# Hybrid encoder trunk on one core: two-half score products, recurrent scans one per attention step, post-norms with the gain first

## The chip, the cores and the metric

The kernel runs on one core of a Trainium2 chip. The core has a matrix engine (TensorE, "PE" in the profile, with its weight loads as "PEld"), three engines for elementwise work (VectorE "DVE", ScalarE "ACT", GpSimd "POOL"), a fifth engine that issues transfers (SyncE "SP"), an on-chip memory of 128 partitions (SBUF) and eight accumulation banks of 128 x 512 floats that PE writes (PSUM). The metric is the device time of one execution in microseconds. Three runs of the kernel before took 1062.80 to 1063.61 us, median 1063.17.

## The reference

An encoder of two layers, 512 tokens of 1024 channels, all in float32. Every layer does `x += post_norm(mixer(pre_norm(x)))` and then `x += post_norm(SwiGLU(pre_norm(x)))`, with RMS norms. Layer 0 mixes by differential attention beside a recurrent branch, layer 1 by a two-dimensional Fourier transform and a linear map. The parts that the change touches:

```python
def rmsnorm(x, g):
    y = x * rsqrt(mean(x * x, axis=-1) + EPS) * g

def diff_attention(q, k, v, lam, ...):       # 4 heads, two 64-wide parts each
    s = einsum('bqhmd,bkhmd->bhmqk', qi, k) * 64 ** -0.5
    p = softmax(s - slopes * dist, axis=-1)
    a = p[:, :, 0] - lam * p[:, :, 1]        # then a @ v and a norm per head

def rg_lru(x, w_a, b_a, w_i, b_i, lam, reverse):   # forward and backward, 512 channels
    r, i = sigmoid(gate products of x)
    a = exp(8 * r * log_sigmoid(lam))
    u = sqrt(1 - a * a) * (i * x)
    h = scan(h = a * h + u)                  # along the 512 positions

rec = (h_fwd + h_bwd) * gelu(yg)
out = concat([attn, rec]) @ w_out
```

## The kernel before

Every large product is made from split operands. A float32 tensor is divided into a high part with a short mantissa (a cast) and a low part (the rest, a subtraction), and a product is three matrix products: high by high, high by low and low by high (`mm3`, lines 108 to 111). `split` (lines 100 to 106) makes the two parts, by default with the cast on ACT and the subtraction on DVE. The weights come as "units" of 256 columns or rows, two halves of 512 KB each: a transfer into one of three raw buffers on SP's queue, a cast, a subtraction (`prep_half`). For units 8 to 13 the subtraction is on POOL. All large tiles, weights included, share 33 slots of 4 KB a partition.

The order in which each engine works is not the program's. A planner orders the instructions of every engine by a priority that follows the program's order, with its own estimate of when operands are ready and slots come free; `order_after` adds an edge that only fixes the order. All engines then work through their queues in order.

Layer 0 goes as follows. After the first norm come the products for the values, the recurrent branch's input with its convolution, and the gates. `lru_decay` (lines 503 to 514) and `lru_root` (518 to 521) make the scans' two inputs for 8 pairs of direction and channel block; the last multiplication of each is on POOL (line 521). `proj_qk(0)` (lines 538 to 567) makes queries and keys of heads 0 and 1, each in four halves of 12 products. A head's query product is a bank whose partitions 0 to 63 hold part 0 and partitions 64 to 127 part 1.

In the kernel before, the split of queries and keys stacks the parts. For queries and each part m, one tile holds the high part in the 64 partitions of m and the low part in the other 64 (lines 555 to 557). For keys, one tile holds the high part twice, and a third tile `klo` holds the low part (lines 561 to 565). A score block is then, for each of the two parts, one product over 128 rows (high by high plus low by high) and one over 64 rows (high by low), lines 582 and 583.

The attention runs in 16 steps, head by head, four blocks of 128 queries each (lines 712 to 722). A step does `scores`; half of a projection (`next(fill)`: queries and keys of heads 2 and 3 in steps 0 to 7, the GELU branch's input in steps 8 to 15); two scans in each of steps 0 to 3; and in `finish_step` the transposes of the mixed probabilities of two steps earlier, the product with the values for a pair of older blocks, and the norm of an older head. In `scores`, DVE scales the bank, adds the position bias and takes the row maximum in one operation (line 585), negates the maximum (587), ACT takes the exponent with the sum (588), and DVE mixes the two parts (592). The backward scan of a channel block is followed by a sum on POOL (line 530); `take_yg`, after the steps, uses that sum.

`proj_tok` makes the products whose result has tokens in the partitions (the mixers' output and the FFN's second product), block by block, with `finish` after each block. There `post_norm` (lines 256 to 267) squares both halves on ACT with a row sum, forms the root's argument on DVE and the root on POOL (`inv_rms`, `inv_sqrt`), and then does per half a product with root and gain (line 266) and the sum into x (line 267) on DVE. In the last FFN, `after1` sends both halves of a finished block to memory from SP.

Of the kernel before, what the change touches and what calls it, by code (L numbers as in the profile page):

```python
# [16 lines left out]
P = 128  # L17
D = 1024
S = 512
# [16 lines left out]
def encoder_kernel(  # L36
# [167 lines left out]
    make_identity(nc, ident)  # L204
    mhalf = const.tile([P, 4], F32, name="mhalf")
    V.memset(mhalf, -0.5)

    def inv_sqrt(m):
        r = sm("r")
        G.tensor_tensor(out=r, in0=m, in1=mhalf[:, 0:1], op=ALU.pow)  # L210
        return r

    def inv_rms(ssa, ssb, n):

        m0, m = sm("m"), sm("m")
        V.tensor_scalar(out=m0, in0=ssa, scalar1=n * EPS, scalar2=None, op0=ALU.add)
        V.tensor_scalar(out=m, in0=ssb, scalar1=m0, scalar2=1.0 / n, op0=ALU.add, op1=ALU.mult)  # L217
        return inv_sqrt(m)

    def pre_stats(t, junk):  # L220
        ss = [sm("ss"), sm("ss")]
        for h in range(2):
            A.activation(junk[h], xt[t][:, h * S:(h + 1) * S], AF.Square, accum_out=ss[h])
        return inv_rms(ss[0], ss[1], D)
# [31 lines left out]
    def post_norm(t, ps, g):  # L256
# [3 lines left out]
        for h in range(2):  # L260
            A.activation(ys[h], ps[h], AF.Square, accum_out=ss[h])  # L261
        r = inv_rms(ss[0], ss[1], D)
        for h in range(2):
            sl = slice(h * S, (h + 1) * S)
            y = ys[h]
            V.scalar_tensor_tensor(out=y, in0=ps[h], scalar=r, in1=g[:, sl], op0=ALU.mult, op1=ALU.mult)
            V.tensor_tensor(out=xt[t][:, sl], in0=xt[t][:, sl], in1=y, op=ALU.add)
# [255 lines left out]
    def lru_scan(d, c):  # L523
        a_, q, u = lru_ac.pop((d, c))
        if d == 0:
            V.tensor_tensor_scan(out=u, data0=a_, data1=u, initial=0.0, op0=ALU.mult, op1=ALU.add)
            hsum[c] = u
        else:
            V.tensor_tensor_scan(out=u[:, ::-1], data0=a_[:, ::-1], data1=u[:, ::-1], initial=0.0, op0=ALU.mult, op1=ALU.add)
# [8 lines left out]
    def proj_qk(h0):  # L538

        qh = {}  # L540
        for z in range(2):
            u = next_unit(1)
            for h in (h0, h0 + 1):
# [8 lines left out]
                a = pair("qk", F32R)  # L552
                if z == 0:

                    for m, sl in enumerate(halves):
                        A.copy(a[m][sl, :], ps[sl, :])
                        V.tensor_tensor(out=a[m][halves[1 - m], :], in0=ps[sl, :], in1=f(a[m][sl, :]), op=ALU.subtract)
                    qh[h] = a
                else:

                    lo = tile1k("klo", F32R)[:, 0:S]
                    for m, sl in enumerate(halves):
                        A.copy(a[m][sl, :], ps[sl, :])
                        A.copy(a[m][halves[1 - m], :], ps[sl, :])
# [391 lines left out]
```

## Time and profile before

| what | value |
|---|---|
| median of three runs | 1063.17 us (1062.80 to 1063.61) |
| the profiled execution's own time | 1063.37 us |
| its span, first to last instruction | 1061.6 us |
| PE busy | 1040.4 us (98%) |
| DVE busy | 487.3 us (46%) |
| ACT busy | 391.7 us (37%) |
| POOL busy | 99.4 us (9%) |
| transfers | 102.40 MB, mean 96 GB/s |

The profile shows one execution. A group of instructions is named by its source line, engine and operation, then output and inputs by the program's names; after the bar come busy time and the mean duration in ns, then idle time ahead of it and what ended that. Matrix products are pipelined: their listed durations overlap, so the distance from start to start tells what one costs. A table of stages gives, per stretch of time, each engine's busy microseconds with the number of its instructions in brackets, then the share of full TensorE clock that was granted, the busy share of the DMA engines and the transfer rate.

### The profile page before, as it was taken

Reading aid. Unit: us, or ns where it says so; the run is one execution under the profiler, and the core shown is the slowest. Engines: PE = TensorE matmul, PEld = TensorE weight load, DVE = VectorE, ACT = ScalarE, POOL = GpSimd, SP = SyncE. Lnnn points to the kernel's source line nnn. Section 1 sums busy time; section 2 is a strip of 40 time slices with the busy share of each in tenths; the row PEclk is TensorE's granted clock in tenths of the full one; section 3 lists DMA queues with packets and bytes.
Section 4 is the critical chain, followed back from the end, with each engine's and each line's share of the span. In section 5 each row is a group of like instructions: output and inputs, shape, how many; then the busy total and the mean of one; then the engine's idle time right before and its main releaser. Section 6 shows DMA issues by size and latency. Waiting matters only on the chain.

```text
span 1061.6 us, 12308 instructions
## 1 busy us (share of the span) xinstructions
PE 1040.4 (98%) x4927; PEld 862.0 (81%) x4927; DVE 487.3 (46%) x763; ACT 391.7 (37%) x645; POOL 99.4 (9%) x94
## 2 busy tenths in 40 slices
PE   8997999999999999999999999999999999999997
PEld 7885677779888888888888888898888888888885
DVE  6869987755542322223324456545322223234304
ACT  5377567743531321122223445334321123223202
POOL 1057424211000000000100110100000000000000
PEclk9998999999999999999999999999999999999999
DMA  6432212321652243222443015027243223324002
GB/s 218 125 103 91 75 48 75 117 80 41 179 177 80 80 135 103 80 80 79 152 127 119 1 60 159 1 70 221 88 126 111 80 79 105 94 80 128 11 1 79
DMA packets 72981, 102.40 MB, mean 96 GB/s; under 512 B 3878, under 2 KB 61275, under 8 KB 72924
## 3 DMA queue, kind: packets, MB, share of 16 engines
q1 hardware_dynamic: 70298, 93.49, 28.2%
q0 software_dynamic: 2624, 8.13, 2.3%
q8 instruction: 38, 0.62, 0.2%
q14 instruction: 19, 0.16, 0.0%
q10 hardware_dynamic: 2, 0.00, 0.0%
HBM read 99.51 MB, written 2.10 MB: 96 GB/s over the span
## 4 chain that ended last, share of the span: by engine, by line
PE 86%; DVE 8%; ACT 3%; issue 1%; DMA 1%; POOL 0%; SPq 0%; DVEq 0%; POOLq 0%; ACTq 0%
PE pc L109 15%; PE pc L110 15%; PE pc L111 15%; PE pj L111 10%; PE pj L110 10%; PE pj L109 10%; DVE wlo L106 2%; ACT gate L93 1%; PE psc L583 1%; DVE xc L430 1%; PE pyg L109 1%; DMA raw<-in_w_in_dram 1%; PE pT L251 1%; PE psc L582 1%; PE put L110 1%
## 5 line engine op out<-in xcount | busy, mean ns | idle before, releaser
L106 DVE TENSOR_TENSOR wlo<-raw,whi 128x1024 fp32r<-128x1024 f32 x158 | 191.8, 1238 | 269.9 <-ACT whi L103 218.3
L110 PE MATMUL pc<-hnlo,whi 128*128 128x512 f32 (+1 forms) x768 | 285.2, 372 | 0.0
L109 PE MATMUL pc<-hnhi,whi 128*128 128x512 f32 (+1 forms) x768 | 284.6, 372 | 0.5 <-ACT hnhi L103 0.5
L111 PE MATMUL pc<-hnhi,wlo 128*128 128x512 f32 (+1 forms) x768 | 285.0, 371 | 0.0
L103 ACT CAST whi<-raw 128x1024 fp32r<-128x1024 f32 x164 | 167.3, 1050 | 116.7 <-PE pj L110 31.1
L110 PEld LDWEIGHTS pc<-hnlo,whi 128*128 128x128 f32 x768 | 144.7, 188 | 25.5 <-DVE hnlo L106 0.4
L109 PEld LDWEIGHTS pc<-hnhi,whi 128*128 128x128 f32 x768 | 144.2, 188 | 25.7 <-ACT hnhi L103 1.0
L111 PEld LDWEIGHTS pc<-hnhi,wlo 128*128 128x128 f32 x768 | 144.7, 188 | 24.9
L109 PE MATMUL pj<-whi,gs 128*128 128x512 f32 x352 | 136.9, 389 | 0.0
L111 PE MATMUL pj<-whi,gs 128*128 128x512 f32 x352 | 136.9, 389 | 0.0
L110 PE MATMUL pj<-wlo,gs 128*128 128x512 f32 x352 | 136.9, 389 | 0.0
L93 ACT ACTIVATE gated<-pc 128x512 f32<-128x512 f32 x44 | 26.2, 597 | 271.6 <-PE pc L111 271.6
L753 DVE TENSOR_TENSOR gated<-gated,pc 128x512 f32<-128x512 f32 x44 | 30.2, 686 | 112.3 <-PE pc L111 112.3
L110 PEld LDWEIGHTS pj<-wlo,gs 128*128 128x128 f32 x352 | 66.1, 188 | 13.8
L109 PEld LDWEIGHTS pj<-whi,gs 128*128 128x128 f32 x352 | 66.1, 188 | 13.8
L111 PEld LDWEIGHTS pj<-whi,gs 128*128 128x128 f32 x352 | 66.1, 188 | 13.5
L210 POOL TENSOR_TENSOR r<-m,mhalf 128x1 f32<-128x1 f32 x32 | 17.4, 545 | 551.0 <-DVE m L217 544.5
L261 ACT ACTIVATE y<-pj 128x512 f32<-128x512 f32 x32 | 19.1, 596 | 82.3 <-PE pj L111 82.3
L103 ACT CAST gs<-gated 128x512 fp32r<-128x512 f32 x44 | 25.3, 619 | 52.2 <-PE pj L110 32.2
L106 DVE TENSOR_TENSOR gs<-gated,gs 128x512 fp32r<-128x512 f32 x44 | 28.4, 685 | 31.0 <-ACT gs L103 31.0
L106 POOL TENSOR_TENSOR wlo<-raw,whi 128x1024 fp32r<-128x1024 f32 x12 | 29.5, 2471 | 49.7 <-ACT whi L103 48.6
L93 ACT ACTIVATE p<-p,mx 128x512 f32<-128x512 f32 x32 | 23.1, 723 | 22.4 <-DVE mx L587 22.3
(199 smaller groups left out, 1299.3 us busy)
## 6 DMA issues: line engine op xcount, KB each, us to landing
raw<-in_w_ffn_gate_dram SPq DMA_DIRECT2D x44, 512.0 KB, 4.6
raw<-in_w_ffn_up_dram SPq DMA_DIRECT2D x44, 512.0 KB, 5.0
raw<-in_w_ffn_down_dram SPq DMA_DIRECT2D x44, 512.0 KB, 3.3
raw<-in_w_in_dram SPq DMA_DIRECT2D x20, 512.0 KB, 4.6
raw<-in_w_mix_out_dram SPq DMA_DIRECT2D x8, 512.0 KB, 3.2
raw<-in_w_fourier_out_dram SPq DMA_DIRECT2D x8, 512.0 KB, 3.7
pos<-in_dft_pos_dram POOLq DMA_DIRECT2D x8, 256.0 KB, 6.3
out_dram<-x SPq DMA_DIRECT2D x8, 256.0 KB, 2.1
```

The source lines that it names most:

```text
L93: ins = A.activation(out_, in_, func, **kw)
L103: A.copy(hi, src)
L106: lo_eng.tensor_tensor(out=lo, in0=src, in1=f(hi), op=ALU.subtract)
L109: T.matmul(ps, lhsT=l[0], rhs=r[0], start=start, stop=False)
L110: T.matmul(ps, lhsT=l[0], rhs=r[1], start=False, stop=False)
L111: T.matmul(ps, lhsT=l[1], rhs=r[0], start=False, stop=stop)
L210: G.tensor_tensor(out=r, in0=m, in1=mhalf[:, 0:1], op=ALU.pow)
L251: T.transpose(pt[:, k * P:(k + 1) * P], xh[:, k * P:(k + 1) * P], ident)
L261: A.activation(ys[h], ps[h], AF.Square, accum_out=ss[h])
L430: V.scalar_tensor_tensor(out=y[:, o], in0=ps[:, i_], scalar=cw[:, k * 4 + c:k * 4 + c + 1], in1=y[:, o], op0=ALU.mult, op1=ALU.add)
L582: T.matmul(ps, lhsT=q_[m][:, t * P:(t + 1) * P], rhs=k_[m], start=True, stop=False)
L753: V.tensor_tensor(out=gated[fc], in0=gated[fc], in1=ps, op=ALU.mult)
```

## The change

Queries and keys are split like every other operand: one cast on ACT and one subtraction on DVE over all 128 partitions, no third tile. The score block becomes six products over 64 rows. For each of the three terms, the product of part 0 (partitions 0 to 63) is followed by that of part 1 (partitions 64 to 127), and the two parts accumulate in two banks taken together. The reduction takes a negative scale and the minimum, so that the exponent can use the result without the negation.

Of the scans, one is done in each of steps 1, 2, 4, 5, 7, 8, 10 and 11, with an edge that puts it behind the last score reduction made so far on DVE.

The root's argument gets its 1/D by the scale of the square. `post_norm` multiplies by the gain first, from the bank, and then does one operation per half that multiplies by the root and adds x. The square's elementwise output goes to a fixed tile, `junk`. The second half of every output block is issued from ACT's queue.

```diff
+    RD = 1.0 / math.sqrt(D)
+    def inv_rms(ssa, ssb):
+        m0, m, r = sm("m"), sm("m"), sm("r")
+        V.tensor_scalar(out=m0, in0=ssa, scalar1=EPS, scalar2=None, op0=ALU.add)
+        V.tensor_tensor(out=m, in0=ssb, in1=m0, op=ALU.add)
         G.tensor_tensor(out=r, in0=m, in1=mhalf[:, 0:1], op=ALU.pow)
...
         for h in range(2):
-            A.activation(ys[h], ps[h], AF.Square, accum_out=ss[h])
-        r = inv_rms(ss[0], ss[1], D)
+            V.tensor_tensor(out=ys[h], in0=ps[h], in1=g[:, h * S:(h + 1) * S], op=ALU.mult)
+            A.activation(junk, ps[h], AF.Square, scale=RD, accum_out=ss[h])
+        r = inv_rms(ss[0], ss[1])
         for h in range(2):
             sl = slice(h * S, (h + 1) * S)
-            y = ys[h]
-            V.scalar_tensor_tensor(out=y, in0=ps[h], scalar=r, in1=g[:, sl], op0=ALU.mult, op1=ALU.mult)
-            V.tensor_tensor(out=xt[t][:, sl], in0=xt[t][:, sl], in1=y, op=ALU.add)
+            V.scalar_tensor_tensor(out=xt[t][:, sl], in0=ys[h], scalar=r, in1=xt[t][:, sl], op0=ALU.mult, op1=ALU.add)
...
+            sc = V.tensor_tensor_scan(out=u, data0=a_, data1=u, initial=0.0, op0=ALU.mult, op1=ALU.add)
...
+        order_after(sc, [last_score[0]])
+        if d:
             G.tensor_tensor(out=hsum[c], in0=hsum[c], in1=u, op=ALU.add)
...
                 a = pair("qk", F32R)
+                split(*a, ps)
                 if z == 0:
-                    for m, sl in enumerate(halves):
-                        A.copy(a[m][sl, :], ps[sl, :])
-                        V.tensor_tensor(out=a[m][halves[1 - m], :], in0=ps[sl, :], in1=f(a[m][sl, :]), op=ALU.subtract)
                     qh[h] = a
                 else:
-                    lo = tile1k("klo", F32R)[:, 0:S]
-                    for m, sl in enumerate(halves):
-                        A.copy(a[m][sl, :], ps[sl, :])
-                        A.copy(a[m][halves[1 - m], :], ps[sl, :])
-                        V.tensor_tensor(out=lo[sl, :], in0=ps[sl, :], in1=f(a[m][sl, :]), op=ALU.subtract)
-                    qks[h] = (qh[h], a, lo)
+                    qks[h] = (qh[h], a)
...
+        ps = [bank("psc"), bank("psc")]
+        for n, (i, j) in enumerate(((0, 0), (0, 1), (1, 0))):
+            for m, sl in enumerate(halves):
+                T.matmul(ps[m], lhsT=q_[i][sl, t * P:(t + 1) * P], rhs=k_[j][sl, :], start=n == 0, stop=n == 2)
         for m in range(2):
-            sl = halves[m]
-            ps = bank("psc")
-            T.matmul(ps, lhsT=q_[m][:, t * P:(t + 1) * P], rhs=k_[m], start=True, stop=False)
-            T.matmul(ps, lhsT=q_[m][sl, t * P:(t + 1) * P], rhs=klo[sl, :], start=False, stop=True)
-            mx = sm("mx")
-            V.tensor_tensor_reduce(out=pr[m], in0=ps, in1=bias[h][:, 384 - t * P:384 - t * P + S],
-                                   op0=ALU.add, op1=ALU.max, scale=1.0 / math.sqrt(QK), scalar=-3.0e38, accum_out=mx)
-            V.tensor_scalar(out=mx, in0=mx, scalar1=-1.0, scalar2=None, op0=ALU.mult)
-            act(pr[m], pr[m], AF.Exp, "exp", bias=mx, accum_out=s_[:, m * NT + t:m * NT + t + 1])
+            mn = sm("mn")
+            last_score[0] = V.tensor_tensor_reduce(out=pr[m], in0=ps[m], in1=bias[h][:, 384 - t * P:384 - t * P + S],
+                                   op0=ALU.add, op1=ALU.min, scale=-1.0 / math.sqrt(QK), scalar=3.0e38, accum_out=mn)
+            act(pr[m], pr[m], AF.Exp, "exp", scale=-1.0, bias=mn, accum_out=s_[:, m * NT + t:m * NT + t + 1])
...
+    scans = list(lru)
     for i in range(n):
...
-        if 2 * i < len(lru):
-            lru_scan(*lru[2 * i])
-            lru_scan(*lru[2 * i + 1])
+        if i % 3 and scans:
+            lru_scan(*scans.pop(0))
...
-        for h in range(2):
-            nc.sync.dma_start(out[t * P:(t + 1) * P, h * S:(h + 1) * S], xt[t][:, h * S:(h + 1) * S])
+        for h, q in enumerate((nc.sync, A)):
+            q.dma_start(out[t * P:(t + 1) * P, h * S:(h + 1) * S], xt[t][:, h * S:(h + 1) * S])
```

More of the change, by code (lines that the diff above doesn't have):

```diff
@@ L204, in encoder_kernel @@
     make_identity(nc, ident)
+    junk = const.tile([P, S], F32, name="junk")
     mhalf = const.tile([P, 4], F32, name="mhalf")
     V.memset(mhalf, -0.5)
-    def inv_sqrt(m):
-        r = sm("r")
+    RD = 1.0 / math.sqrt(D)
[3 more added lines that the diff above has]
+        V.tensor_tensor(out=m, in0=ssb, in1=m0, op=ALU.add)
         G.tensor_tensor(out=r, in0=m, in1=mhalf[:, 0:1], op=ALU.pow)
         return r
[L213 to L218, printed above, removed]
     def pre_stats(t, junk):
@@ L222, in pre_stats @@
         for h in range(2):
-            A.activation(junk[h], xt[t][:, h * S:(h + 1) * S], AF.Square, accum_out=ss[h])
-        return inv_rms(ss[0], ss[1], D)
+            A.activation(junk[h], xt[t][:, h * S:(h + 1) * S], AF.Square, scale=RD, accum_out=ss[h])
+        return inv_rms(ss[0], ss[1])
     hn = {}
@@ L525, in lru_scan @@
         if d == 0:
-            V.tensor_tensor_scan(out=u, data0=a_, data1=u, initial=0.0, op0=ALU.mult, op1=ALU.add)
+            sc = V.tensor_tensor_scan(out=u, data0=a_, data1=u, initial=0.0, op0=ALU.mult, op1=ALU.add)
             hsum[c] = u
         else:
-            V.tensor_tensor_scan(out=u[:, ::-1], data0=a_[:, ::-1], data1=u[:, ::-1], initial=0.0, op0=ALU.mult, op1=ALU.add)
+            sc = V.tensor_tensor_scan(out=u[:, ::-1], data0=a_[:, ::-1], data1=u[:, ::-1], initial=0.0, op0=ALU.mult, op1=ALU.add)
+        order_after(sc, [last_score[0]])
+        if d:
             G.tensor_tensor(out=hsum[c], in0=hsum[c], in1=u, op=ALU.add)
@@ L570, in encoder_kernel @@
     sums = {}
+    last_score = [None]
     def scores(h, t):
-        q_, k_, klo = qks[h]
+        q_, k_ = qks[h]
         pr = pair("p")
```

## The prediction

> **What bounds the kernel now.** I read the page's engine totals and the chain of waits first.
>
> ```profile
> PE 1040.4 (98%) x4927; PEld 862.0 (81%) x4927; DVE 487.3 (46%) x763; ACT 391.7 (37%) x645; POOL 99.4 (9%) x94
> ...
> PE 86%; DVE 8%; ACT 3%; issue 1%; DMA 1%; POOL 0%; SPq 0%; DVEq 0%; POOLq 0%; ACTq 0%
> ```
>
> The matrix engine (PE) has work in 98% of the span and carries 86% of the chain. So only two things can move the time: a stretch where PE stands still, or fewer PE microseconds where it is dense. The table of stages shows where it stands still.
>
> ```profile
> core 0: us, PE busy (x) PEld busy (x) DVE busy (x) ACT busy (x) POOL busy (x), PEclk, DMA share, GB/s
> 85.00:95.00 10.00, 10.00 (x45) 8.07 (x43) 9.88 (x14) 9.58 (x16) 8.35 (x5) 1.00 0.19 53
> 95.00:105.00 10.00, 3.50 (x9) 1.96 (x8) 9.91 (x8) 3.83 (x7) 10.00 (x5) 0.74 0.17 53
> 105.00:115.00 10.00, 10.00 (x28) 6.09 (x28) 9.94 (x13) 5.59 (x9) 5.80 (x4) 0.75 0.17 53
> 115.00:125.00 10.00, 8.52 (x34) 5.59 (x33) 9.07 (x20) 3.54 (x8) 4.70 (x4) 1.00 0.39 144
> ```
>
> Up to 95 us PE is dense. From 95 to 125 it runs 9, 28 and 34 instructions in 10 us each, against 45 before, while VectorE (DVE) is busy 9.9, 9.9 and 9.1 of 10 us; the granted clock falls to 0.74 (before 1.00). The attention's sixteen steps (a step is one head and one block of 128 queries) begin at 94.74; step 4 begins at 125.90 and the last of the 32 full score products (two a step) starts at 191.0 (first and last start in the second fence below). The same table cut there, with two later stages:
>
> ```profile
> 94.74:125.90 31.16, 22.70 (x74) 14.06 (x72) 30.07 (x40) 13.67 (x25) 20.76 (x12) 0.84 0.24 82
> 125.90:190.60 64.70, 64.70 (x312) 47.99 (x309) 49.15 (x136) 44.77 (x96) 22.00 (x10) 1.00 0.21 66
> 225.00:265.00 40.00, 39.76 (x243) 35.30 (x242) 21.81 (x44) 14.62 (x37) 4.98 (x9) 1.00 0.09 27
> 680.00:710.00 30.00, 29.76 (x208) 27.53 (x207) 14.79 (x30) 9.42 (x23) 2.75 (x5) 1.00 0.06 18
> ```
>
> So DVE bounds steps 0 to 3 (30.07 of 31.16 us); in steps 4 to 15 PE is dense and DVE at 76%. PE's longest wait between 90 and 230 us, and the start of the first step:
>
> ```profile
> PE psc L583 <- DVE klo L565: 5.8, 2, 3.2
> ```
>
> ```profile
> 94.74 0.39 PE L582 MATMUL psc<-qk,qk 128*128 128x512 f32 x1
> 98.38 0.50 PE L583 MATMUL psc<-klo,qk 64*128 64x512 f32 x1 [3.25 <-DVE klo L565]
> ...
> 125.90 0.47 PE L582 MATMUL psc<-qk,qk 128*128 128x512 f32 x1
> ```
>
> ```profile
> L582 PE MATMUL psc<-qk,qk x32: 388/494/628, 94.7 to 191.0; 128*128 128x512 f32 x32
> ```
>
> PE starts the first score product at 94.74 and gets the second at 98.38, waiting for the low part of the keys (klo) on DVE. What fills DVE there:
>
> ```profile
> L526 DVE TENSOR_TENSOR_SCAN gate<-gate 128x512 f32<-128x512 f32 x4 | 8.8, 2196 | 0.0
> ...
> L529 DVE TENSOR_TENSOR_SCAN gate<-gate 128x512 f32<-128x512 f32 x4 | 7.2, 1797 | 0.0
> ...
> L585 DVE CUSTOM_DVE_ANT_0 p<-psc,bias 128x512 f32<-128x512 f32 x6 | 4.0, 682 | 0.1
> L592 DVE SCALAR_TENSOR_TENSOR p<-p,c 128x512 f32<-128x512 f32 x2 | 3.6, 1795 | 0.0
> ...
> L565 DVE TENSOR_TENSOR klo<-pqk,qk 64x512 fp32r<-64x512 f32 x4 | 2.8, 688 | 0.1
> ...
> L587 DVE TENSOR_SCALAR mx<-mx 128x1 f32<-128x1 f32 x6 | 0.9, 144 | 0.0
> ```
>
> ```profile
> L526 DVE TENSOR_TENSOR_SCAN gate<-gate x4: 1199/2260/3062, 95.3 to 111.7; 128x512 f32<-128x512 f32 x4
> ```
>
> The eight recurrent scans (L526, L529) take 8.8 + 7.2 = 16.0 us, half of the stretch. One takes 1.2 us at best, 2.2 mostly; GpSimd (POOL) works in most of that time:
>
> ```profile
> 86.65 16.33 POOL L521 TENSOR_TENSOR gate<-gate,th 128x512 f32<-128x512 f32 x8 [8.01 <-ACT th L93]
> 102.94 3.42 POOL L530 TENSOR_TENSOR gate<-gate,gate 128x512 f32<-128x512 f32 x2
> 106.31 2.38 POOL L106 TENSOR_TENSOR wlo<-raw,whi 128x1024 fp32r<-128x1024 f32 x1
> ```
>
> And the score block of step 9, on PE:
>
> ```profile
> 154.81 0.60 PE L604 MATMUL paT<-ident,p 128*128 128x128 f32 x4
> 155.17 0.48 PE L582 MATMUL psc<-qk,qk 128*128 128x512 f32 x1
> 155.58 0.50 PE L583 MATMUL psc<-klo,qk 64*128 64x512 f32 x1
> 156.01 0.50 PE L582 MATMUL psc<-qk,qk 128*128 128x512 f32 x1
> 156.44 0.50 PE L583 MATMUL psc<-klo,qk 64*128 64x512 f32 x1
> 156.87 0.50 PE L109 MATMUL pyg<-hnhi,whi 128*128 128x512 f32 x1
> 157.21 0.39 PE L110 MATMUL pyg<-hnlo,whi 128*128 128x512 f32 x1
> 157.43 0.39 PE L111 MATMUL pyg<-hnhi,wlo 128*128 128x512 f32 x1
> ```
>
> Full products follow each other at 0.22 to 0.23 us (157.21 to 157.43). The four score products of a step alternate between 128 and 64 rows, and each start comes 0.41 to 0.43 after the one before; the product behind them is late too (0.34). From 155.17 to 157.21 are 2.04 us for five products, 1.15 at 0.23: 0.89 us goes to four changes of shape, 0.22 each, and a step's score block costs 2.04 - 0.23 = 1.81 us.
>
> **The change, part by part.** The sum is made against the profiled execution: 1063.37 us, of which 1061.6 is span and 1.77 lies around it; the median of the runs is 1063.17, 0.2 lower.
>
> *Score products.* Six products of 64 rows replace two full and two of 64 rows, in the order upper half, lower half, three times. The trace has no two 64-row products of different halves next to each other, so the block is bounded by rows. Two changes of shape remain (in and out, 0.22 each: 0.44). Low end: the halves run together and each pair costs a full product, 3 x 0.23 + 0.44 = 1.13 us, 0.68 less than now. If a pair runs together but the next load on the same half stays exposed, as the loads at 155.58 to 156.44 are, a pair costs 0.43: 3 x 0.43 + 0.11 (the rest of the way out, 0.34 - 0.23) = 1.40, 0.41 less. Nothing together, loads hidden: 6 x 0.23 + 0.44 = 1.82, the same as now. High end: nothing together and every load exposed: 6 x 0.43 + 0.11 = 2.69, 0.88 more. I take 1.27, between the first two, since both halves of the array are free for each other and write different banks.
>
> The Trainium skill, TensorE: Matmul & The Clock Gate, Part 3, says that a weight load overlaps a running product only where the row groups differ. The loads of full products above do overlap (the next product starts after 0.23), so the trace limits that rule; by it the block would be 1.40, by the rows of full products 1.13, and the sum below 1.6 us worse or better over twelve steps.
>
> *Splits of queries and keys.* Per head, DVE goes from four 64-partition operations (0.69 each, L565; a full-width one costs the same) to two, ScalarE (ACT) from six copies to two. Before 94.74 PE is dense, so that part only shortens DVE's backlog; the keys' low part is then one operation, due before PE ends the projections. The wait of 3.2 us at 98.38 and its twin (5.8 in two) lose their cause.
>
> *Scans.* Two at each of steps 0 to 3 become one at each of steps 1, 2, 4, 5, 7, 8, 10, 11, each behind that step's score reductions on DVE. Behind a scan now stand the step's exponent mix (L592) and the transposed copies, which PE wants two steps later. The backward scans' sums on POOL (102.94, two in 3.42) move with them: the low parts of the next key weights (106.31), behind them on POOL until now, come earlier; the gates that want the sums come after step 15, four steps after the last one. No DMA is issued by a moved operation. The backward gates' four tiles, of 33 that the weights share, stay until step 11 instead of 3, while the four of the keys' low parts are no longer taken: even.
>
> *Negations.* L587 (0.14 each, 32 of them) goes; ACT takes the sign into its scale. It is DVE time and a link between reduction and exponent.
>
> *Steps 0 to 3.* PE needs 4 x 1.27 + 48 projection products x 0.23 = 11.0 + two groups of transposes of 0.36 = 16.8 us. DVE keeps 30.1 - 16.0 = 14.1, gets two scans at 2.0 (POOL's multiplications run to 103) = 4.0 and one more step's reductions and mix (2 x 0.68 + 0.70, L592 undisturbed, as L266 below) = 2.1, and loses three splits of 0.69 and six negations (0.9) = 3.0: 17.2. Two engines near 17 with hand-overs between them make about 19: **12.2 us saved** of 31.2. Bounds: 14.9 (PE alone at block 1.13: 16.3) and 6 (a first turn that still waits, 25).
>
> *Steps 4 to 15.* PE falls by 12 x 0.54 = 6.5 from 64.7 to 58.2. DVE falls from 49.2 by two key splits, one query split (2.1) and 24 negations (3.5) to 43.6 and gets six scans at 1.2 to 2.2; POOL is busy a third of the time (22.0 of 64.7), so 1.55: 9.3, together 52.9. All scans lie in steps 4 to 11, where DVE has 8/12 of 43.6 + 9.3 = 38.4 against PE's 38.8. So near a tie costs something: I give back 1.5 us. **5.0 saved**; bounds 8.2 and, at block 2.69, a loss of 10.6.
>
> *Post-norms.* The order of multiplications changes, so that one DVE operation per half is left after the root in place of two. In the three inner ones PE's products cover it: PE lacks 0.24 us in each of the stages at 225 and 680 above, so nothing is gained, and if the cover went it would be a gain of 1.3 each at most. The last one is bare:
>
> ```profile
> 1051.19 0.60 ACT L261 ACTIVATE y<-pj 128x512 f32<-128x512 f32 x1 [1.97 <-PE pj L111]
> ...
> 1051.50 1.28 DVE L267 TENSOR_TENSOR x<-x,y 128x512 f32<-128x512 f32 x2
> ...
> 1053.97 0.60 ACT L261 ACTIVATE y<-pj 128x512 f32<-128x512 f32 x1 [2.09 <-PE pj L111]
> ...
> 1055.62 1.41 DVE L266 SCALAR_TENSOR_TENSOR y<-pj,r,gpost 128x512 f32<-128x512 f32 x2 [0.72 <-POOL r L210]
> 1056.95 1.28 DVE L267 TENSOR_TENSOR x<-x,y 128x512 f32<-128x512 f32 x2
> ```
>
> After the root (1055.62) four operations end at 1058.23; two, at 0.64 to 0.70 each, end at 1056.9: **1.3 us saved**. The early multiplications fit in the 2.7 us between the two squares (1051.19, 1053.97).
>
> *Output on two queues.* Half of each block now goes out from ACT's queue, whose one DMA issue in the trace took 0.50 us:
>
> ```profile
> 0.73 0.50 ACTq L130 DMA_DIRECT2D grow<-in_ln_mix_pre_dram  x1
> ```
>
> Behind that issue, which waits for DVE (1052.78 for block 2), stands ACT's square of the next block (1051.19); it may be late by a microsecond, covered by the one at 1053.97, which ends the block. The halves come 0.64 us apart, so a second queue has nothing to overlap: 0, bounds -0.6 and +0.5.
>
> Sum: 12.2 + 5.0 + 1.3 = 18.5; 1063.4 - 18.5 = **1045 us**.
>
> **Rivals.** (1) The halves do not run together, loads hidden: block 1.82. Steps 0 to 3: PE 19.0, about 20.2 with hand-overs, 11 saved; steps 4 to 15 nothing; tail 1.3: 1051. For it: no row shows concurrent products. Against it: nothing in the program ties the halves.
> (2) DVE becomes the bound through step 11, the scans at 2.2 with POOL beside them: a scan step needs 43.6/12 + 2.2 = 5.8 us against PE's 4.85, six times 0.98 = 5.9 in place of my 1.5, and about 3 more at the start, where hand-overs then follow each scan: 18.5 - 4.4 - 3 = 11.1, 1052. For it: the median scan of 2.26. Against it: POOL's busy third.
> (3) Slower: every 64-row load stays exposed, block 2.69, because the array empties at each change of half as at each change of shape now. Steps 0 to 3: 22.5 of PE and 3 of hand-overs, 5.6 saved; steps 4 to 15 lose 10.6; tail 1.3: +3.7, **1067**. The sign turns at a block of 2.46 (at x the change is 4x - 16.4 + 12x - 21.7 - 1.3). For it: all the exposed loads above. Against it: those follow a change between whole array and half.
> (4) The change doesn't reach the queue: the planner's order still puts other DVE work ahead of the first reductions, and steps 0 to 3 save 6 only: 1051.
>
> **How the numbers follow.** Forecast 0.58, (1) 0.15, (2) 0.1, (3) 0.07, (4) 0.1. The forecast's own spread is 1039 (14.9 + 8.2 + 1.3 = 24.4) to 1050; (1), (2) and (4) lie at 1051 and 1052, and (1) with the bound of 6 at the start comes to 1056. Range **1039 to 1057**. Faster by over 0.2% (2.1 us, about what a measurement tells from no change) 0.89, all but (3) less 0.04 for mixtures of it that end within 0.2%; slower 0.07.
>
> **What would show it.** In the table of stages, PE dense from 95 us on, the clock at 1.00, step 4 starting near 114 and step 15 ending near 173. In the timeline of a dense step, six score products with the pair's starts close together and a block of 1.1 to 1.4 us. No wait of PE for the keys' low part. Scans one at a time behind L585, DVE at 90% of those steps. Two DVE operations after the last root. I am wrong if the block is 1.8 or more, or if PE shows waits for DVE or for free banks in steps 1 to 11.

## The result and the profile after

The changed kernel takes 1050.84 us (median of four runs, 1050.56 to 1051.33) against 1063.39 us (1062.80 to 1064.03) beside it: a ratio of 0.9882 with a 95% interval of 0.9865 to 0.9899. The profiled execution took 1050.92 us, of which 1049.1 is span: 12.5 less than the 1061.6 of before. First the engine totals and the chain of the page after.

```profile
PE 1031.0 (98%) x4959; PEld 857.8 (82%) x4959; DVE 477.8 (46%) x723; ACT 382.1 (36%) x629; POOL 96.2 (9%) x94
...
PE 88%; DVE 6%; ACT 3%; issue 1%; DMA 1%; POOL 1%; SPq 0%; POOLq 0%; DVEq 0%; ACTq 0%
```

They hardly differ from those of before: PE has 9.4 us less work, and 88% of the chain. The table of stages, in three slices of the prediction, says where the time went.

```profile
95.00:105.00 10.00, 10.00 (x48) 6.75 (x47) 7.75 (x13) 6.92 (x12) 10.00 (x7) 1.00 0.30 87
105.00:115.00 10.00, 10.00 (x52) 7.35 (x50) 8.91 (x21) 4.40 (x13) 2.73 (x4) 1.00 0.44 163
115.00:125.00 10.00, 8.76 (x50) 6.44 (x49) 9.93 (x17) 5.01 (x11) 4.81 (x2) 1.00 0.33 100
```

From 95 to 115 PE runs 48 and 52 instructions where it ran 9 and 28, and the clock stays at 1.00. At 115 the picture turns: PE 8.76 of 10 us, DVE 9.93. The same table cut at the starts of steps 0, 4, 12 and 15, for the kernel before (steps 4, 12, 15) and after (steps 0, 4, 12, 15):

```profile
125.90:172.19 46.29, 46.29 (x223) 34.28 (x221) 36.88 (x103) 32.20 (x70) 11.49 (x5) 1.00 0.14 46
172.19:190.19 18.00, 18.00 (x91) 13.55 (x90) 12.27 (x34) 12.16 (x26) 10.51 (x5) 1.00 0.38 118
```

```profile
94.67:111.31 16.64, 16.64 (x81) 11.63 (x81) 14.03 (x26) 9.41 (x18) 12.69 (x10) 1.00 0.45 153
111.31:157.57 46.26, 42.93 (x237) 32.62 (x236) 40.39 (x83) 26.23 (x60) 14.56 (x8) 1.00 0.15 46
157.57:178.76 21.19, 18.17 (x97) 14.07 (x96) 16.03 (x32) 13.39 (x30) 11.83 (x6) 0.94 0.29 100
```

Steps 0 to 3 took 31.16 us and take 16.64: 14.5 saved. Steps 4 to 11 took 46.29 and take 46.26: nothing saved, though their products are shorter. Steps 12 to 14 took 18.00 and take 21.19: 3.2 lost, at a mean clock of 0.94. From step 15 to the end it was 1061.6 - 190.19 = 871.4 and is 1049.1 - 178.76 = 870.3: 1.1 saved. With 0.1 for the earlier first step these make the 12.5.

The score block itself came out as short as hoped. In PE's timeline of step 1:

```profile
98.60 0.39 PE L111 MATMUL pqk<-hnhi,wlo 128*128 128x512 f32 x1
98.92 0.97 PE L578 MATMUL psc<-qk,qk 64*128 64x512 f32 x6
99.81 0.50 PE L109 MATMUL pqk<-hnhi,whi 128*128 128x512 f32 x1
100.15 0.40 PE L110 MATMUL pqk<-hnlo,whi 128*128 128x512 f32 x1
```

Six products fill 0.97 us. From 98.60 to 100.15 are 1.55 us with two full products in them (L111 and L109, 0.23 each): the block costs 1.09, against 1.81 before. At 0.72 less in each of eleven steps, steps 4 to 14 would have gone from 64.29 to 56.4 us, had nothing else changed. They take 67.45. So 11 us were lost there, and PE's waits between 94 and 180 us name one place:

```profile
PE poT L110 <- DVE aT L106: 6.1, 3, 3.0
```

The waits for the keys' low part are gone. In their place PE waits three times, 3.0 us at the longest, with the product of transposed probabilities and values (`poT`) for DVE's low part of these probabilities (`aT`). The chain of waits from 111 to 178 us, by line, for before and after:

```profile
by line: PE psc L583 11.4%; PE psc L582 8.9%; PE pyg L109 8.4%; PE pyg L111 6.9%; PE pyg L110 6.8%; PE pqk L109 6.7%; PE paT L604 6.2%; PE pqk L110 5.5%; PE pqk L111 5.5%; DVE gate L529 5.1%; DVE p L592 4.3%; DVE p L585 3.9%; PE poT L109 3.
```

```profile
by line: DVE p L588 17.4%; DVE p L582 12.5%; ACT p L93 10.8%; DVE aT L106 9.4%; ACT whi L103 7.0%; DVE gate L525 6.1%; issue 4.7%; POOL r L628 4.4%; DVE c L587 3.7%; POOL wlo L106 3.6%; ACT oT L630 3.4%; DVE s L624 2.7%; DVE qk L106 2.3%; A
```

Before, PE's own products led that chain. After, it is DVE's: the mix (L588) leads with 17.4%, ahead of the score reductions (L582). What the mix does there, in the timelines of POOL, DVE and PE ahead of the two longest of the three waits:

```profile
120.01 2.42 POOL L106 TENSOR_TENSOR wlo<-raw,whi 128x1024 fp32r<-128x1024 f32 x1 [1.25 <-ACT whi L103]
...
120.18 2.79 DVE L588 SCALAR_TENSOR_TENSOR p<-p,c 128x512 f32<-128x512 f32 x1
...
126.07 1.32 POOL L532 TENSOR_TENSOR gate<-gate,gate 128x512 f32<-128x512 f32 x1 [3.65 <-DVE c L586]
...
126.27 1.67 DVE L588 SCALAR_TENSOR_TENSOR p<-p,c 128x512 f32<-128x512 f32 x1
...
128.46 0.68 DVE L106 TENSOR_TENSOR aT<-paT,aT 128x512 fp32r<-128x512 f32 x1
...
129.19 0.39 PE L110 MATMUL poT<-aT,v 128*128 128x256 f32 x1 [2.02 <-DVE aT L106]
...
167.34 7.06 POOL L106 TENSOR_TENSOR wlo<-raw,whi 128x1024 fp32r<-128x1024 f32 x3 [2.19 <-ACT whi L103]
...
172.15 2.81 DVE L588 SCALAR_TENSOR_TENSOR p<-p,c 128x512 f32<-128x512 f32 x1
...
174.88 0.68 DVE L106 TENSOR_TENSOR aT<-paT,aT 128x512 fp32r<-128x512 f32 x1
...
175.61 0.39 PE L110 MATMUL poT<-aT,v 128*128 128x256 f32 x1 [3.02 <-DVE aT L106]
```

A mix takes 0.75 us alone. Here two take 2.79 and 2.81, and end at 122.97 and 174.96: 0.54 and 0.56 us after POOL's subtraction of weights has ended (122.43 and 174.40). The one between them takes 1.67, beside one of POOL's sums. Behind the mixes on DVE stand the subtractions of the transposed probabilities: PE waits 2.02 us for the one at 128.46 (step 6) and 3.02 for the one at 174.88 (step 14). The third wait, 1.10 us in step 4 (at 116.88), ends the same kind of row, in which DVE also waits 0.98 us for the exponents.

Going by the starts of the steps, and with 0.72 less for each than before, four steps hold nearly all of the 11 us: 1.9 in step 4, 2.4 in step 6, 0.9 in step 10 and 5.1 in step 14. The other seven lose about 0.1 each.

### The profile page after: what moved, and what is told of

It is laid out like the page before. It is cut to its first block, busy times and chain, and to the rows that moved or that the text cites. A ratio compares the mean times of both kernels' runs of the same rounds, so it can differ in the third digit from the quotient of the medians.

```text
span 1049.1 us, 12316 instructions
## 1 busy us (share of the span) xinstructions
PE 1031.0 (98%) x4959; PEld 857.8 (82%) x4959; DVE 477.8 (46%) x723; ACT 382.1 (36%) x629; POOL 96.2 (9%) x94
## 4 chain that ended last, share of the span: by engine, by line
PE 88%; DVE 6%; ACT 3%; issue 1%; DMA 1%; POOL 1%; SPq 0%; POOLq 0%; DVEq 0%; ACTq 0%
PE pc L110 15%; PE pc L109 15%; PE pc L111 15%; PE pj L111 10%; PE pj L110 10%; PE pj L109 10%; DVE p L588 1%; DVE p L582 1%; ACT whi L103 1%; PE pT L251 1%; ACT p L93 1%; PE pqk L109 1%; DVE aT L106 1%; DMA raw<-in_w_in_dram 1%; PE put L109 1%
## 5 line engine op out<-in xcount | busy, mean ns | idle before, releaser
L109 PE MATMUL pc<-hnhi,whi 128*128 128x512 f32 (+1 forms) x768 | 284.6, 372 | 0.5 <-ACT hnhi L103 0.5
L111 PE MATMUL pc<-hnhi,wlo 128*128 128x512 f32 (+1 forms) x768 | 284.9, 371 | 0.0
L109 PEld LDWEIGHTS pc<-hnhi,whi 128*128 128x128 f32 x768 | 144.2, 188 | 26.0 <-ACT hnhi L103 1.0
L111 PEld LDWEIGHTS pc<-hnhi,wlo 128*128 128x128 f32 x768 | 144.7, 188 | 24.6
L109 PE MATMUL pj<-whi,gs 128*128 128x512 f32 x352 | 136.9, 389 | 0.0
L111 PE MATMUL pj<-whi,gs 128*128 128x512 f32 x352 | 136.9, 389 | 0.0
L109 PEld LDWEIGHTS pj<-whi,gs 128*128 128x128 f32 x352 | 66.1, 188 | 13.8
L111 PEld LDWEIGHTS pj<-whi,gs 128*128 128x128 f32 x352 | 66.1, 188 | 13.7
L262 ACT ACTIVATE junk<-pj 128x512 f32<-128x512 f32 x32 | 19.2, 599 | 94.9 <-DVE y L261 57.8
L261 DVE TENSOR_TENSOR y<-pj,gpost 128x512 f32<-128x512 f32 x32 | 22.0, 689 | 56.6 <-PE pj L111 56.5
L93 ACT ACTIVATE p<-p,mn 128x512 f32<-128x512 f32 x32 | 22.9, 719 | 31.1 <-DVE mn L582 27.9
```

The source lines that it names most:

```text
L93: ins = A.activation(out_, in_, func, **kw)
L109: T.matmul(ps, lhsT=l[0], rhs=r[0], start=start, stop=False)
L111: T.matmul(ps, lhsT=l[1], rhs=r[0], start=False, stop=stop)
L261: V.tensor_tensor(out=ys[h], in0=ps[h], in1=g[:, h * S:(h + 1) * S], op=ALU.mult)
L262: A.activation(junk, ps[h], AF.Square, scale=RD, accum_out=ss[h])
```

## The experiments

All times are medians; the kernel before took 1063.27 to 1063.66 us on the same chip beside them.

**The three parts one at a time, on the kernel before.** First the scans alone:

```diff
-        if 2 * i < len(lru):
-            lru_scan(*lru[2 * i])
-            lru_scan(*lru[2 * i + 1])
+        if i % 3 and scans:
+            lru_scan(*scans.pop(0))
```

> The kernel before with the scans alone moved: one in each of steps 1, 2, 4, 5, 7, 8, 10, 11, behind the step's score reductions. Theory (the eight scans on VectorE are what starved the first steps): with a score block of 1.81 us steps 0 to 3 are about 20 to 21 us on the matrix engine in place of 31.2, steps 4 to 15 stay dense at 64 to 66, so 1052 to 1054 us, and step 4 starts near 115. Rival (the split of queries and keys, with its waits of PE for the keys' low part, holds the start as much as the scans): 6 us saved at most, 1057 or more, with waits of PE for klo still in the trace.

Measured: 1062.52 us, ratio 0.9993 (0.9984 to 1.0002): no change that can be told. The theory's time is missed and the rival's range holds, though PE's waits for the keys' low part come to 1.1 us only. The stages of this run, cut at steps 0, 4 and 15, show what happened.

```profile
94.72:116.82 22.10, 20.30 (x73) 13.17 (x72) 16.22 (x42) 13.90 (x27) 12.68 (x9) 0.92 0.36 117
116.82:189.13 72.31, 68.11 (x312) 49.53 (x310) 58.61 (x134) 43.21 (x92) 25.45 (x13) 0.95 0.17 53
```

Steps 0 to 3 fall to 22.10 us, 9.1 saved as the theory said. Steps 4 to 14 rise from 64.29 to 72.31, and 8.0 are given back. DVE has 58.61 us of work there where it had 49.15; one of the scans takes 3.43 us, beside POOL's subtractions. The products are the old, longer ones here, so the scans alone are enough to make these steps late.

Then the scores alone: splits, six products, no negation, with two scans in each of steps 0 to 3 as before.

```diff
-            T.matmul(ps, lhsT=q_[m][:, t * P:(t + 1) * P], rhs=k_[m], start=True, stop=False)
-            T.matmul(ps, lhsT=q_[m][sl, t * P:(t + 1) * P], rhs=klo[sl, :], start=False, stop=True)
+        for n, (i, j) in enumerate(((0, 0), (0, 1), (1, 0))):
+            for m, sl in enumerate(halves):
+                T.matmul(ps[m], lhsT=q_[i][sl, t * P:(t + 1) * P], rhs=k_[j][sl, :], start=n == 0, stop=n == 2)
```

> The kernel before with the splits, the six paired products and the missing negation alone; two scans stay in each of steps 0 to 3. Theory: the block falls to about 1.1 us in every step, but VectorE still bounds steps 0 to 3, which save 3 to 5 us; steps 4 to 15 save part of 12 x 0.7 = 8.4, the rest turns into waits of PE for the transposed probabilities: 1052 to 1057 us. If the scans inside steps 4 to 11 are what costs the waits in the changed kernel, steps 4 to 15 save all of 8 here (step 4 to step 15 in about 57 us); if it is the order and POOL's subtractions, they save 3 or less.

Measured: 1059.73 us, ratio 0.9965 (0.9952 to 0.9978), a miss of the 1052 to 1057. The waits of PE between 94 and 180 us, and the stage of steps 4 to 14:

```profile
PE paT L598 <- DVE p L586: 10.8, 1, 10.8
...
125.80:186.63 60.83, 58.76 (x331) 45.86 (x330) 44.16 (x103) 39.51 (x87) 21.27 (x10) 0.99 0.23 70
```

Without the spread scans the head isn't shortened at all: step 4 starts at 125.80, as before, after one wait of 10.8 us for the first mix, which stands behind the scans on DVE. Steps 4 to 14 save 3.5 of the 7.9, with no scan among them: they are late without the scans too, by 4.4.

Last the post-norms and the second output queue, with the lines of the change's diff for them.

> The kernel before with the post-norms and the second output queue alone. Theory: only the last norm is on the path, four operations behind the root become two: 1.3 us saved, 1062.1 us. Rival: the three inner norms are on the path as well, 2.5 us or more saved; or nothing, because the second queue's transfer ends later.

Measured: 1062.68 us, ratio 0.9994 (0.9985 to 1.0004), 0.7 less, not clear of no change. Alone the parts give 0.9, 3.7 and 0.7 us, 5.3 together; in one kernel they give 12.5. Neither the shorter PE steps nor the free head is worth much without the other: the first leaves PE waiting for DVE at the head, the second leaves it waiting in steps 4 to 14.

**Do the halves run together?** The products of the changed kernel, half by half in place of alternating:

```diff
-        for n, (i, j) in enumerate(((0, 0), (0, 1), (1, 0))):
-            for m, sl in enumerate(halves):
+        for m, sl in enumerate(halves):
+            for n, (i, j) in enumerate(((0, 0), (0, 1), (1, 0))):
```

> The changed kernel with the six score products ordered part by part (three on the upper half, then three on the lower), all else equal. If neighbours on different halves run together and nothing else matters, the block grows from 1.09 to about 1.8 us (loads hidden) or 2.7 us (each load exposed). With 0.7 more in each of 16 steps: 2.9 us lost in steps 0 to 3; in steps 4 to 15 the product waits less for the transposed probabilities, so 3 to 9 us: 1056 to 1062 us. With loads exposed (1.6 more in each): 1066 us or more. Rival (the halves do not run together, the short block has another cause): 1051, no change.

Measured: 1051.16 us, ratio 0.9882 (0.9868 to 0.9897), the same as the changed kernel, and the time that the rival gave. Its block in PE's timeline:

```profile
99.07 0.97 PE L578 MATMUL psc<-qk,qk 64*128 64x512 f32 x6
```

Six products again fill 0.97 us. So the longer block of the theory didn't come. That left two readings: the halves run together in either order, or a 64-row product is simply cheap. The next kernel tells them apart. It takes both parts from the upper half, so that nothing can run side by side:

```diff
-            for m, sl in enumerate(halves):
+            for m, sl in enumerate((halves[0], halves[0])):
```

> The changed kernel with all six score products of a step on the upper half (the second part is computed from the first part's rows; its output is another one). It tells why the block takes 0.69 us of pairs in either order: if the two halves of the array work side by side, six products on one half take 1.3 us or more, and the block 1.8 or more; if a 64-row product simply costs half of a full one, the block stays at 1.1.

Measured, in a single profiled run: 1053.35 us. Its block, and its stages from step 0 to 4 and from 4 to 15:

```profile
99.36 0.39 PE L111 MATMUL pqk<-hnhi,wlo 128*128 128x512 f32 x1
99.68 1.66 PE L578 MATMUL psc<-qk,qk 64*128 64x512 f32 x6
...
101.60 0.40 PE L110 MATMUL pqk<-hnlo,whi 128*128 128x512 f32 x1
```

```profile
94.74:114.14 19.40, 19.40 (x81) 13.73 (x80) 16.79 (x27) 9.42 (x18) 12.59 (x10) 1.00 0.40 131
114.14:180.17 66.03, 65.50 (x331) 51.33 (x330) 55.15 (x111) 38.99 (x85) 26.12 (x13) 1.00 0.20 65
```

Six products now fill 1.66 us, and the block costs 2.24 - 0.46 = 1.78 (from 99.36 to 101.60, less two full products). So the halves do run side by side in the changed kernel, and in either order of the queue. The second thing this run shows is worth more: the block costs 0.69 more in each of sixteen steps, 11 us of PE, and the time rises by 2.5. At the head it costs in full (19.40 against 16.64). In steps 4 to 14 it costs less than nothing (66.03 against 67.45). There PE isn't the bound.

**What DVE waits for or is slowed by, in steps 4 to 14.** The scans taken out of the changed kernel altogether:

```diff
-            sc = V.tensor_tensor_scan(out=u, data0=a_, data1=u, initial=0.0, op0=ALU.mult, op1=ALU.add)
...
-            sc = V.tensor_tensor_scan(out=u[:, ::-1], data0=a_[:, ::-1], data1=u[:, ::-1], initial=0.0, op0=ALU.mult, op1=ALU.add)
```

> The changed kernel without the eight scans (the recurrent branch then sums the scans' inputs; its output is another one). The changed kernel takes 67.5 us from the start of step 4 to that of step 15, where 64.6 of the kernel before less 11 blocks of 0.72 would be 56.7: 10.8 us are lost. The kernel with the new score products alone, whose scans all lie before step 4, takes 60.8. Theory S (the scans' time on VectorE makes the later steps late): without them 61 us or less, 1044 us or less. Rival O (the order of the queues and POOL's subtractions make them late, the scans only add their part at steps 1 and 2): 65 us or more, 1048 or more.

Measured: 1046.11 us, ratio 0.9846 (0.983 to 0.9862), between the two. The stage from step 4 to 15:

```profile
110.90:173.18 62.28, 58.77 (x331) 45.48 (x331) 46.01 (x107) 39.17 (x86) 22.05 (x12) 0.99 0.28 92
```

Taking out the scans gives back 5.2 of the 11 us. But with 10.4 us less on DVE than in the changed kernel (46.01 against 56.42) the stage is still 62.28 us, 6 above the 56.4. DVE's load alone doesn't explain the loss. Nor is it all that changes here: without the scans one mix of this stage is stretched (to 2.82 us), where four were (2.79, 1.67, 1.67 and 2.81). Next, POOL's part taken away: the low parts of the weight units 9 to 13 are made on DVE, which so gets more work, not less.

```diff
-LO_POOL = (8,9,10,11,12,13)
+LO_POOL = (8,)
```

> The changed kernel with the weight subtractions of units 9 to 13 on VectorE in place of POOL (ten of them in steps 4 to 16). Theory P (VectorE's operations with two operands from memory are stretched while POOL subtracts, the mix from 0.75 to 2.8 us, and that is what PE waits for): the mixes stay at 0.75, the waits for the transposed probabilities shrink, 1046 to 1048 us. Rival S (VectorE's total time is the bound): 10 x 1.24 = 12.4 us more on VectorE against 8 saved in stretched operations, 1053 to 1056 us.

Measured: 1048.72 us, ratio 0.9862 (0.9848 to 0.9877), 2.1 less than the changed kernel: 0.7 above the range of theory P and far below the rival's. From step 4 to 15, for the changed kernel and this one:

```profile
111.31:178.76 67.45, 61.10 (x333) 46.70 (x332) 56.42 (x114) 39.62 (x88) 26.39 (x14) 0.98 0.19 63
```

```profile
111.17:174.67 63.50, 59.80 (x332) 45.66 (x331) 55.06 (x118) 38.61 (x85) 8.16 (x6) 1.00 0.21 67
```

POOL falls from 26.39 to 8.16 us. DVE takes over eight subtractions in this stage and is still busy for less time (55.06 against 56.42), because most of its other operations are no longer stretched; two mixes beside POOL's sums still take 1.67 us. In the whole program DVE gets ten subtractions of 1.22 us, and its busy time rises by 1.6 us only (477.8 to 479.4).

Whether it was the order of work on ACT and DVE that counted was asked twice. The first exponent and the first reduction of a step were put behind the copies of the transposed probabilities:

```diff
+            if last_turn[0] and m == 0:
+                order_after(e, last_turn[0][:1])
+                order_after(last_score[0], last_turn[0][1:])
```

> The changed kernel with two edges a step: the first exponent of a step behind the cast of the transposed probabilities made just before it (ScalarE), the first score reduction behind their subtraction (VectorE). Theory O (those two are ready at the start of the step but stand in the queues behind the step's softmax, so that PE finds them late two or three times): the waits of PE for them (6.1 us) go, with the lowered clock after the longest, 1042 to 1046 us. Rival S (VectorE has no time to spare, the wait only moves): 1049 to 1052 us.

Measured: 1051.20 us, ratio 0.9886 (0.9871 to 0.99). Nothing moves, since the queues had that order already; so the run says nothing on theory O. Then the mix of a step was put behind the reductions of the next one, so that DVE needn't wait for the exponents:

```diff
+        mixes[h, t] = pr
...
         scores(*steps[i])
+        if i:
+            mix(*steps[i - 1])
```

> The changed kernel with the mix of a step's two parts (reciprocal, factor, sum) moved behind the next step's score reductions. In the changed kernel VectorE goes through each step in a row: reductions, about 1 us of waiting for the exponents, mix, the split of queries or keys, the subtraction of the transposed probabilities, and only then the next reductions, which it starts 5 us after PE finished the scores. Theory D (this row, with the wait inside it, is longer than PE's step and is what PE waits for): the waits for exponents go from VectorE, PE's waits for the transposed probabilities (6.1 us) shrink, 1043 to 1047 us. Rival P (the operations that POOL's subtractions stretch are the cause): 1049 us or more.

Measured: 1051.55 us, ratio 0.9888 (0.9874 to 0.9903), a miss of the theory and within rival P. DVE's waits for exponents are gone, but the stretched operations are not, as DVE's timeline and then POOL's show:

```profile
116.98 2.48 DVE L525 TENSOR_TENSOR_SCAN gate<-gate 128x512 f32<-128x512 f32 x1
...
119.38 2.29 DVE L594 SCALAR_TENSOR_TENSOR c<-c,nlam,sums 128x1 f32<-128x1 f32 x1
...
115.97 2.41 POOL L106 TENSOR_TENSOR wlo<-raw,whi 128x1024 fp32r<-128x1024 f32 x1 [5.30 <-ACT whi L103]
118.96 2.69 POOL L106 TENSOR_TENSOR wlo<-raw,whi 128x1024 fp32r<-128x1024 f32 x1 [0.58 <-ACT whi L103]
```

Now a scan (1.2 us alone) takes 2.48 and an operation on one column (0.2 alone) takes 2.29, each beside a subtraction on POOL. The later mix only met POOL with other operations. The two edits together, mix and weight units:

> The kernel with the late mix, and the weight subtractions of units 9 to 13 on VectorE in place of POOL. By theory D the two add: the stretched mixes go as well (2.1 us came from that alone), 1041 to 1045 us. If VectorE has no time left, the 12 us of subtractions cost more than they free: 1047 or more.

Measured: 1047.96 us, ratio 0.9854 (0.9839 to 0.9869), a miss of theory D. The time lies where the rival had it, but the subtractions don't cost more than they free: the units give 3.6 us here against 2.1 alone. Its stage from step 4 to 15:

```profile
110.98:172.06 61.08, 58.93 (x331) 45.51 (x330) 54.02 (x117) 38.39 (x84) 8.25 (x5) 1.00 0.21 69
```

The stage is 2.4 us shorter than with the units alone (63.50), so the late mix shortens it once POOL is quiet. In the whole time it gives 0.8 us, which the intervals don't tell from nothing.

**The tail.** On the kernel with the late mix, the last squares ahead of the last multiplications:

```diff
-            V.tensor_tensor(out=ys[h], in0=ps[h], in1=g[:, h * S:(h + 1) * S], op=ALU.mult)
             A.activation(junk, ps[h], AF.Square, scale=RD, accum_out=ss[h])
         r = inv_rms(ss[0], ss[1])
+        for h in range(2):
+            V.tensor_tensor(out=ys[h], in0=ps[h], in1=g[:, h * S:(h + 1) * S], op=ALU.mult)
```

> The kernel with the late mix, and in the post-norm the square before the multiplication by the gain. In the changed kernel ScalarE's square of the last half waits for VectorE's multiplication on the same bank (the last square starts at 1042.82, 1.0 us after the product ends), so the chain behind the last product holds 0.68 more and 1.3 less than before. With the square first: 0.5 us less than the kernel with the late mix alone. If the square did not wait for the bank but for something else, no change.

Measured: 1050.89 us, ratio 0.988 (0.9864 to 0.9897), 0.66 less than without. The intervals overlap, but the traces show the gain: from the start of the last product to the end of the span it is 7.6 us without (1043.20 to 1050.8) and 6.8 with (1041.98 to 1048.8). The ends of the changed kernel and of this one:

```profile
1042.02 0.69 DVE L261 TENSOR_TENSOR y<-pj,gpost 128x512 f32<-128x512 f32 x1 [1.01 <-PE pj L111]
...
1042.82 0.60 ACT L262 ACTIVATE junk<-pj 128x512 f32<-128x512 f32 x1 [1.04 <-DVE m L215]
```

```profile
1042.49 0.60 ACT L261 ACTIVATE junk<-pj 128x512 f32<-128x512 f32 x1 [2.05 <-PE pj L111]
...
1043.29 0.68 DVE L264 TENSOR_TENSOR y<-pj,gpost 128x512 f32<-128x512 f32 x1
```

In the changed kernel the square doesn't start until the multiplication on the same bank has run, 0.80 us after that one's start. Here it starts 0.51 us after the last product's start, and the multiplication runs beside the root.

**All of it together.** The late mix, the units and the tail, and the sums of the two scan directions moved from POOL to DVE as well:

```diff
-            G.tensor_tensor(out=hsum[c], in0=hsum[c], in1=u, op=ALU.add)
+            V.tensor_tensor(out=hsum[c], in0=hsum[c], in1=u, op=ALU.add)
```

> The changed kernel with three things together: the mix of a step behind the next step's reductions, the subtractions of units 9 to 13 on DVE, and the last square ahead of the last multiplications (1047.96 us with the first two; the third gave 0.66 us). New here: the sums of the two scan directions go from POOL to DVE, so that POOL does nothing but the norms' roots in the attention's steps. If DVE's operations beside POOL's are what is left (theory P), the stretched mixes beside the sums get shorter and PE's waits in steps 4 to 15 fall below the 2.9 us of the run without this: 1045.5 to 1047. If DVE's own load counts (rival), four more operations of about 0.7 us in steps 2 to 11 lengthen the chain and the saving of 0.66 is used up: 1047.5 to 1049.

Measured: **1046.33 us** (1045.52 to 1046.75), ratio 0.984 (0.9824 to 0.9857), within theory P, and 4.5 us below the changed kernel. Its stage from step 4 to 15:

```profile
111.59:171.07 59.48, 58.85 (x331) 45.64 (x331) 53.04 (x120) 38.30 (x84) 3.99 (x2) 1.00 0.22 72
```

Then the durations (least, median, longest, in ns) of the mix, in the changed kernel and in this one:

```profile
L588 DVE SCALAR_TENSOR_TENSOR p<-p,c x16: 741/752/2849, 100.2 to 182.9; 128x512 f32<-128x512 f32 x16
```

```profile
L596 DVE SCALAR_TENSOR_TENSOR p<-p,c x16: 717/750/752, 105.9 to 180.2; 128x512 f32<-128x512 f32 x16
```

POOL is left with 4 us. No mix takes more than 0.752 us where the longest took 2.849, and the stage falls from 67.45 to 59.48 us (in steps: 63.50 with the units, 61.08 with the late mix, 59.48 with the sums, each from one profiled execution), though in the whole program ten subtractions and four sums more lie on DVE than in the changed kernel. Of the 11 us 3.1 stay lost. And not all of the 8.0 reaches the end: from step 15 on this kernel takes 1043.6 - 171.07 = 872.5 us, 2.2 more than the changed one. PE's wait for ACT's normed attention output in that part is longer, 2.3 us in place of 0.6.

## Why the prediction was right, and where its sum was wrong

The direction and the range held, and the block and the head did better than was taken. The time came out 5.8 us above the 1045: steps 4 to 15 are 8.2 us short of the sum, and the head gives 2.3 more than its term. The time alone says little, since rivals (1), (2) and (4) lay at 1051 and 1052; the stages decide. By the prediction's own sign, waits of PE for DVE in steps 1 to 11, it was wrong in a part: PE waits for DVE in steps 4 and 6 (1.10 and 2.02 us).

*Score products.* The block was taken as 1.27 and bounded below at 1.13; it measures 1.09. The reason given, halves running together, is shown by 0.97 us for six against 1.66 on one half. The Trainium skill, TensorE: Matmul & The Clock Gate, Part 3, says that weight loads overlap a running product only where the row groups differ; the 1.40 that this would have made is not what ran, and even the six products on one half started closer together (1.66 us for six) than the exposed loads of 0.43 each would allow.

*Steps 0 to 3.* 12.2 predicted, 14.5 measured, beside the bound of 14.9. The 2.2 us for hand-overs between two engines near their limits was too much: DVE is busy 14.03 us there and not 17.2, since it runs a step behind PE. The scores of step 3 are reduced only after PE has begun step 4 (111.31):

```profile
112.15 0.68 DVE L582 CUSTOM_DVE_ANT_0 p<-psc,bias 128x512 f32<-128x512 f32 x1
```

What was booked as a gain at the head so came back as a debt in the next stage.

*Steps 4 to 15.* This is the step that failed: "near a tie costs something: I give back 1.5 us", 5.0 saved. Measured are 3.2 lost, and 11 us lie between the stage and its shorter products. DVE's work was counted well: 14.03 and 56.42 us in the two stages, 70.5 together, where 17.2 and 52.9 were predicted. What failed is the comparison of sums behind the 1.5, 38.4 us of DVE against 38.8 of PE. DVE goes through each step in one row (mix, copies, two reductions, scan), and a stretched operation in it holds the copy that PE wants next; the term has no price for that. Where the sum set a price for a mix, at the head, it took it as "undisturbed", though the row quoted for it showed a mean of 1.795 us for two. And step 4 in the timelines of POOL and DVE before had this:

```profile
131.34 5.20 POOL L106 TENSOR_TENSOR wlo<-raw,whi 128x1024 fp32r<-128x1024 f32 x2 [11.49 <-ACT whi L103]
...
131.72 2.55 DVE L592 SCALAR_TENSOR_TENSOR p<-p,c 128x512 f32<-128x512 f32 x1
```

So the price stood in the trace of before. There it lay under PE's products, and no wait of PE followed it (64.29 of 64.29 us busy in steps 4 to 14). The scans and the products both took from that cover: the scans alone, which give DVE more work, lose 8.0 us in these steps, and the shorter products alone, which give PE less, fall 4.4 short. After the longest wait the clock falls too (0.94 in steps 12 to 14, 1.00 before).

That the stretched operations are a cause is shown by the runs that quiet POOL: with the units alone moved the stage falls by 4.0 us, though DVE takes over eight subtractions of 1.22; with the late mix and the sums as well, where every mix is back at 0.75 us, it falls by 8.0 to 59.48. How much of the loss is DVE's plain load isn't told apart from this, since without the scans both the load and the stretching are less. The Trainium skill, SBUF — State Buffer, section "SBUF: two separate sides", says that VectorE and GpSimd share one pair of memory ports, locked for a whole instruction, which a VectorE operation needs when it has two inputs in SBUF. The trace agrees: mixes, scans and even one-column operations, all with two inputs from SBUF, end behind POOL's operation, while the score reductions, with one input from an accumulation bank, take the same in the changed kernel and in the last one, by their groups from 94 to 192 us:

```profile
L582 DVE CUSTOM_DVE_ANT_0 p<-psc,bias 128x512 f32<-128x512 f32 x32 | 20.8, 681 | 0.2 <-PE psc L578 0.2
```

```profile
L583 DVE CUSTOM_DVE_ANT_0 p<-psc,bias 128x512 f32<-128x512 f32 x32 | 20.9, 685 | 2.6 <-PE psc L579 2.6
```

*Rivals.* Rival (2), DVE as the bound through step 11, named the right engine and the right partner, POOL. Its price isn't borne out, and that its 1052 lies near the measured time is in part luck. It priced a step with a scan at 5.8 us; the six of them take 5.6 on average, but the longest, step 6 with 8.00 us (123.14 to 131.14), has no scan of its own. It had the scans at 2.2 us, and five of the six in this stage take 1.2; it is mostly the mixes that are stretched. Its 3 us at the head didn't come, and the loss went on in steps 12 to 14, where no scan is left. Rivals (1) and (3) fall with the block of 1.09, rival (4) with the dense head.

*Post-norms.* 1.3 predicted. From the start of the first operation behind the last product to the end of the span it was 7.6 us (1053.97 to 1061.6) and is 7.1 (1042.02 to 1049.1). The two operations fewer are there; the claim that "the early multiplications fit in the 2.7 us between the two squares" is what failed, for the last of them runs ahead of the square on the same bank. The tail's run, with the square first, ends 0.66 us earlier. Nothing was gained or lost in the three inner ones, as said; PE lacks 0.24 us in such a stage after the change too:

```profile
230.00:270.00 40.00, 39.76 (x277) 36.91 (x277) 20.10 (x31) 16.98 (x30) 3.36 (x6) 1.00 0.30 88
```

The second output queue shows no gain or loss of note: from the end of DVE's last operation to the end of the span it was 3.4 us (1058.23 to 1061.6) and is 3.3 (1045.83 to 1049.1).

What stays open: the waits by name come to 6.1 of the 11 us, and the rest isn't divided by cause. Of the 5.1 in step 14, 3.0 are the wait, and behind it the granted clock is 0.51 from 176.00 to 178.76. What holds the last kernel's stage 3.1 us above the 56.4 is open too, as is why a part of its gain is lost after step 15. A greater distance between transposes and products with the values would test that the copy's lateness is all that counts; no run tries it.

## What to carry to other kernels

Before PE's work in a stage is shortened, look at the longest, not only the median, durations of the operations that it covers: a stretched operation that is free under PE's products becomes the bound when they shrink, or when its own engine gets more work in the same stage. An elementwise operation moved to GpSimd isn't free where VectorE works on SBUF operands at the same time; here, giving VectorE more work and leaving GpSimd idle was faster. And parts of a change that relieve different engines in turn should be priced together: alone these gave 5.3 us, together 12.5.

## What was unexpected of the hardware

Products on the two halves of the array run side by side whether the queue alternates between them or holds three of one half and then three of the other (0.97 us for six either way, 1.66 on one half). A one-column operation on VectorE takes 2.29 us in place of 0.2 beside a subtraction on GpSimd: the loss goes by GpSimd's operation, not by the size of VectorE's.
